# Last row group of a batch: one VectorE sum and one transposing matmul in place of nine accumulating matmuls

## The chip, the cores and the metric

The kernel runs on one core of a Trainium2 chip. Times are device microseconds of one execution. A run is one such time; beside it stands the span of an execution of that run, from its first to its last recorded instruction, and the mean TensorE clock that the records grant. "Tail" means here the last 10 us of the span, in which the last loads land and the final matmuls, scans and output run.

## The reference

`x` has 8 batches of 2048 rows of 4096 numbers, `w` has 4096.

```python
proj = (x @ w).squeeze(-1)                    # 8 x 2048 dot products
cm = np.maximum.accumulate(proj, axis=1)      # running maximum
is_record = (proj >= cm).astype(np.float32)
return np.cumsum(is_record, axis=1)           # running count of records
```

## The kernel before

268 MB of x are streamed once. VectorE (DVE) multiplies and sums the first 2816 columns of each row itself; GpSimd (POOL) multiplies the rest and ScalarE (ACT) sums it. TensorE (PE) adds the partial sums and turns them from a column (one row of x per partition) into a row (one batch per partition) by a matmul against the identity, accumulating in one PSUM tile `ps`. Then three VectorE operations make the maximum, the compare and the count.

The last 128 rows of batch 0 come in seven column pieces of falling size, so that little work is left when the last one lands. Each piece leaves its own 128x1 partial sum (the two pieces that POOL shares leave two).

```python
    PIECES = [   # batch, columns loaded, VectorE's columns, GpSimd's columns
        (1, 1408, D, (1408, VC), (VC, D)),
        (1, 0, 1408, (0, 1408), None),
        (0, 2816, D, (2816, 3328), (3328, D)),          # piece 2
        (0, 2048, 2816, (2048, 2816), None),
        (0, 1280, 2048, (1600, 2048), (1280, 1600)),    # piece 4
        (0, 832, 1280, (832, 1280), None),
        (0, 448, 832, (448, 832), None),
        (0, 160, 448, (160, 448), None),
        (0, 0, 160, (0, 160), None),                    # piece 8
    ]
    ...
        for i, (b, c0, c1, v, p) in enumerate(PIECES):
            ...
            piece(slot(B - 1 - b)[1], v, p, dst_v, dst_p, xq[i])
            if i == 1:
                parts += [(B, st_v, (sd, nv)), (B, b1x, None), (B, st_p, (pa, na))]
            elif b == 0:
                parts.append((1, dst_v, (sd, nv)))
                if p:
                    parts.append((1, dst_p, (pa, na)))

        a0 = next(i for i, q in enumerate(parts) if q[2] == (pa, na - 1))
        a1 = next(i for i, q in enumerate(parts) if q[2] == (pa, na))
        parts.insert(len(parts) - 2, parts.pop(a1))
        parts.insert(len(parts) - 4, parts.pop(a0))
        for k, (m, l, wait) in enumerate(parts):
            i = T.matmul(
                out=ps[:m, :P], lhsT=l[:, :m], rhs=identity,
                start=k == 0, stop=k == len(parts) - 1,
            )
            if wait:
                i._wait_ge(*wait)
        i.then_inc(psr, 1)
        scans(cm_l, rec_l, cnt_l, P, cm[:, N - 1 :], cnt[:, N - 1 :], 4)
        SY.dma_start(out=out[:, S0:], in_=cnt_l)._wait_ge(cs, NG + 2).then_inc(oe, 16)
```

TensorE's order of the twelve final parts is: three for all batches, then of batch 0 the pieces 2, 3, 4, 5, 6 (VectorE), piece 2 (ScalarE), piece 7, piece 4 (ScalarE), piece 8. `sd` counts VectorE's dots, `pa` ScalarE's sums.

Of the kernel before, what the change touches and what calls it, by code (L numbers as in the profile page):

```python
# [13 lines left out]
ALU = mybir.AluOpType  # L14
# [6 lines left out]
def kernel(  # L21
# [31 lines left out]
    PIECES = [  # L53
        (1, 1408, D, (1408, VC), (VC, D)),
        (1, 0, 1408, (0, 1408), None),
        (0, 2816, D, (2816, 3328), (3328, D)),
        (0, 2048, 2816, (2048, 2816), None),
        (0, 1280, 2048, (1600, 2048), (1280, 1600)),
# [3 lines that stand above are left out]
# [28 lines left out]
    def cut(n):  # L90
        off[0] += n
        assert off[0] <= 352
        return small[:, off[0] - n : off[0]]
# [1 line left out]
    sum_v, sum_p = cut(R * B), cut(R * B)  # L95
    st_v, st_p = cut(B), cut(B)
    b1x = cut(B)
    acc_v = cut(len(PIECES))
    acc_p = cut(len(PIECES))
    neg = cut(1)[:B]  # L100
    zero = ps[:B, WC - 1 :]

# [2 lines left out]
    def sem(name):  # L105
        return tc.alloc_semaphore(f"{name}_{next(ns)}")
# [6 lines left out]
    ws, idn, bw, wc, cs, od, oe, psr, pd, pl, go, sd, pa, con = (  # L113
        sem(n) for n in "ws idn bw wc cs od oe psr pd pl go sd pa con".split()
    )

    V, A, G, T, SY = nc.vector, nc.scalar, nc.gpsimd, nc.tensor, nc.sync

    def dot(xsl, wsl, dst):
        return V.tensor_tensor_reduce(  # L120
            out=xsl, in0=xsl, in1=wsl, scale=1.0, scalar=0.0,
            op0=ALU.mult, op1=ALU.add, accum_out=dst,
        )

    def add_up(xsl, dst):
        return A.activation(out=xsl, in_=xsl, func=ACTF.Copy, accum_out=dst)  # L126

    def w_pool(c0, c1):
        if c0 >= VC:
            return w_sb[:, c0 - VC : c1 - VC]  # L130
        assert W2 <= c0 and c1 <= W2 + WC
        return w2[:, c0 - W2 : c1 - W2]
# [15 lines left out]
    with tc.tile_critical(no_gpsimd_drain=True):  # L148

        for k in range(NK):  # L150
            g, t = divmod(k, B)
            i = SY.dma_start(
                out=xbuf[k % NS],
                in_=x[B - 1 - t, g * N : (g + 1) * N, :].rearrange(
                    "(p r) d -> p (r d)", r=R
                ),
            ).then_inc(xs[k % NS], 16)
            if k >= NS:
                i._wait_ge(fr[k % NS], 2 * (k // NS))
            if k == 0:  # L160
                A.dma_start(
                    out=w_row, in_=w.rearrange("(k c) one -> k (c one)", k=NW)
                ).then_inc(ws, 16)
            if t == NS and g:
                SY.dma_start(
                    out=out[:, (g - 1) * N : g * N], in_=cnt
                )._wait_ge(cs, g + 1).then_inc(od, 16)

        def slot(m):
            return m // R, xbuf[m // R][:, (m % R) * D : (m % R + 1) * D]  # L170
# [14 lines left out]
        for i, (b, c0, c1, _, _) in enumerate(PIECES):  # L185
            row_load(B - 1 - b, c0, c1, b, xq[i])
            if i == 3:
                SY.dma_start(
                    out=out[:, (NG - 1) * N : S0], in_=cnt
# [5 lines left out]
            out=identity, in_=identity, compare_op=ALU.not_equal, fill=1.0,  # L195
# [7 lines left out]
        for n, k in enumerate(order):  # L203
            c = k * WC
            dst = w_v[:, c : c + WC] if c < CV else ps
            i = T.matmul(  # L206
                out=dst, lhsT=identity[:NW, k : k + 1].to_broadcast([NW, P]),
                rhs=w_row, start=True, stop=True,
            ).then_inc(bw, 1)
# [21 lines left out]
        with V.Fori(0, NG):  # L231
# [3 lines left out]
            for t in range(B):  # L235
                b, s = B - 1 - t, t % NS
                V.wait_ge(xs[s], 16).then_inc(go, 1)
                V.sem_inc(xs[s], -16)  # L238
                for j in range(R):
                    i = dot(  # L240
                        xbuf[s][:, j * D : j * D + VC], w_v[:, :VC],
                        sum_v[:, j * B + b : j * B + b + 1],
                    )
# [3 lines left out]
        with G.Fori(0, NG):  # L247
            for t in range(B):
                s = t % NS
                for j in range(R):  # L250
                    xl = xbuf[s][:, j * D + VC : (j + 1) * D]
                    i = G.tensor_mul(out=xl, in0=xl, in1=w_sb).then_inc(pl, 1)  # L252
# [4 lines left out]
        with A.Fori(0, NG):  # L257
            for t in range(B):
                b, s = B - 1 - t, t % NS
                for j in range(R):  # L260
                    i = add_up(
                        xbuf[s][:, j * D + VC : (j + 1) * D],
                        sum_p[:, j * B + b : j * B + b + 1],
                    )._wait_ge(pl, j + 1)
# [5 lines left out]
        for g in range(NG):  # L270
            for j in range(R):
                for k, l in enumerate((sum_p, sum_v)):
                    i = T.matmul(  # L273
                        out=ps[:B, j:N:R], lhsT=l[:, j * B : (j + 1) * B],
                        rhs=identity, start=k == 0, stop=k == 1,
                    )
# [6 lines left out]
        nv = npool = na = 0  # L283
        parts = []

        def piece(xb, v, p, dst_v, dst_p, landed):
            nonlocal nv, npool, na
            dot(xb[:, v[0] : v[1]], w_v[:, v[0] : v[1]], dst_v)._wait_ge(
                landed, 16
            ).then_inc(sd, 1)  # L290
            nv += 1
            if p:
                xl = xb[:, p[0] : p[1]]
                G.tensor_mul(out=xl, in0=xl, in1=w_pool(*p))._wait_ge(  # L294
                    landed, 16
                ).then_inc(pl, 1)
                npool += 1
                add_up(xl, dst_p)._wait_ge(pl, npool).then_inc(pa, 1)
                na += 1
# [8 lines left out]
        for i, (b, c0, c1, v, p) in enumerate(PIECES):  # L308
            if b == 1:
                dst_v, dst_p = (b1x if p is None else st_v)[:, 1:2], st_p[:, 1:2]  # L310
            else:
                dst_v, dst_p = acc_v[:, i : i + 1], acc_p[:, i : i + 1]
            piece(slot(B - 1 - b)[1], v, p, dst_v, dst_p, xq[i])
            if i == 1:
                parts += [(B, st_v, (sd, nv)), (B, b1x, None), (B, st_p, (pa, na))]
            elif b == 0:
                parts.append((1, dst_v, (sd, nv)))
                if p:
                    parts.append((1, dst_p, (pa, na)))

        a0 = next(i for i, q in enumerate(parts) if q[2] == (pa, na - 1))
        a1 = next(i for i, q in enumerate(parts) if q[2] == (pa, na))
        parts.insert(len(parts) - 2, parts.pop(a1))
        parts.insert(len(parts) - 4, parts.pop(a0))
        for k, (m, l, wait) in enumerate(parts):
            i = T.matmul(  # L326
                out=ps[:m, :P], lhsT=l[:, :m], rhs=identity,
                start=k == 0, stop=k == len(parts) - 1,
            )
# [36 lines left out]
```

## Time and profile before

| | before |
|---|---|
| time, median of 3 runs | 631.44 us (631.29 to 631.71) |
| span of the profiled execution | 630.1 us |
| HBM traffic | 268 MB at 426 GB/s |
| busy: VectorE, GpSimd, TensorE | 64%, 59%, 5% |
| last dot's end to the cummax scan, in this trace | 1.70 us |

The timeline of the kernel before, at the end (start, length, engine, line, operation, output<-inputs, shapes, count, and in brackets the idle time before and who ended it). PEld is the weight load that goes with each pass of a matmul; an fp32 matmul here is two passes (24 recorded for the twelve final ones):

```profile
620.19 5.71 PE L326 MATMUL ps<-identity,small 128*8 128x128 f32 x24 [22.85 <-DVE small L120]
...
623.68 1.79 PEld L326 LDWEIGHTS ps<-identity,small 128*1 128x1 f32 x10 [0.39 <-DVE small L120]
...
623.92 0.32 DVE L120 CUSTOM_DVE_ANT_0 xall<-xall,w_v 128x160 f32<-128x160 f32 x1
624.16 0.08 DVE L120 DVE_READ_ACCUMULATOR2_ANT small<- 128x1 f32 x1
625.94 0.47 DVE L135 TENSOR_TENSOR_SCAN cm_l<-ps,cm,small 8x128 f32<-8x128 f32 x1 [1.70 <-PE ps L326]
626.45 0.28 DVE L139 TENSOR_TENSOR rec_l<-ps,cm_l 8x128 f32<-8x128 f32 x1
626.76 0.47 DVE L142 TENSOR_TENSOR_SCAN cnt_l<-rec_l,cnt,ps 8x128 f32<-8x128 f32 x1
627.26 0.31 SPq L334 DMA_DIRECT2D out_dram<-cnt_l  x1
```

The last dot is over at 624.24, but the scan starts 1.70 us later. In between PE works off a backlog: ten weight loads, so ten passes, so five matmuls, stand in a row from 623.68 on. Single passes taken from the trace start 0.213 us apart.

### The profile page before, as it was taken

Reading aid. Unit: us, or ns where it says so; the run is one execution under the profiler, and the core shown is the slowest. Engines: PE = TensorE matmul, PEld = TensorE weight load, DVE = VectorE, ACT = ScalarE, POOL = GpSimd, SP = SyncE. Lnnn points to the kernel's source line nnn. Section 1 sums busy time; section 2 is a strip of 40 time slices with the busy share of each in tenths; the row PEclk is TensorE's granted clock in tenths of the full one; section 3 lists DMA queues with packets and bytes.
Section 4 is the critical chain, followed back from the end, with each engine's and each line's share of the span. In section 5 each row is a group of like instructions: output and inputs, shape, how many; then the busy total and the mean of one; then the engine's idle time right before and its main releaser. Section 6 shows DMA issues by size and latency. Waiting matters only on the chain.

```text
span 630.1 us, 1239 instructions
## 1 busy us (share of the span) xinstructions
PE 33.4 (5%) x100; PEld 14.7 (2%) x100; DVE 406.2 (64%) x295; ACT 177.7 (28%) x262; POOL 369.2 (59%) x137
## 2 busy tenths in 40 slices
PE   8000000010000001000000010000001000000103
PEld 3000000000000000000000000000000000000001
DVE  0756666677655557766666675556667766555886
ACT  1322223233232222233232322222232322322332
POOL 0555666666555555666666555556666665555864
PEclk9999999999999999999999999999999999999999
DMA  9999999999999999999999999999999999999995
GB/s 385 415 446 443 412 443 444 422 434 440 424 437 441 431 427 443 440 415 446 438 421 440 440 424 437 440 425 434 440 440 418 443 440 418 444 437 417 425 431 209
DMA packets 8035, 268.55 MB, mean 426 GB/s; under 512 B 936, under 2 KB 1496, under 8 KB 2016
## 3 DMA queue, kind: packets, MB, share of 16 engines
q1 hardware_dynamic: 8016, 268.50, 98.7%
q8 instruction: 1, 0.02, 0.0%
q10 hardware_dynamic: 16, 0.02, 0.0%
q14 instruction: 2, 0.02, 0.0%
HBM read 268.45 MB, written 0.07 MB: 426 GB/s over the span
## 4 chain that ended last, share of the span: by engine, by line
POOL 52%; issue 38%; DMA 6%; PE 3%; DVE 0%; POOLq 0%; ACT 0%; SPq 0%; ACTq 0%
POOL xall L252 52%; DMA xall<-in_x_dram 6%; PE w_v L206 2%; PE ps L326 1%; PE ps L206 0%; DMA w<-in_w_dram 0%; DVE xall L120 0%; POOLq L255 0%; ACT w L216 0%; DVE cm_l L135 0%; DVE cnt_l L142 0%; SPq L176 0%; DVE rec_l L139 0%; ACT xall L126 0%; POOLq L247 0%
## 5 line engine op out<-in xcount | busy, mean ns | idle before, releaser
L120 DVE CUSTOM_DVE_ANT_0 xall<-xall,w_v 128x2816 f32<-128x2816 f32 (+3 forms) x135 | 389.3, 2931 | 185.8 <-DVEq L238 183.8
L252 POOL TENSOR_TENSOR xall<-xall,w_sb 128x1280 f32<-128x1280 f32 x120 | 345.2, 2903 | 246.0 <-POOLq L255 246.0
L126 ACT ACTIVATE xall<-xall 128x1280 f32<-128x1280 f32 x129 | 162.6, 1261 | 430.9 <-POOL xall L252 413.1
L273 PE MATMUL ps<-identity,small 128*8 128x128 f32 x60 | 13.6, 418 | 567.1 <-ACT xall L126 567.1
L294 POOL TENSOR_TENSOR xall<-xall,w_sb 128x1280 f32<-128x1280 f32 (+1 forms) x8 | 22.1, 2765 | 6.7 <-DMA xall<-in_x_dram 6.6
L126 ACT ACTIVATION_READ_ACCUMULATOR xall<-xall 128x1 f32 x129 | 24.0, 186 | 0.0
L273 PEld LDWEIGHTS ps<-identity,small 128*8 128x8 f32 x60 | 7.4, 130 | 574.4 <-ACT xall L126 570.6
L135 DVE TENSOR_TENSOR_SCAN cm<-ps,cm,small 8x384 f32<-8x384 f32 x6 | 6.0, 1004 | 15.0 <-PE ps L273 15.0
L206 PE MATMUL w_v<-w,identity 8*128 8x512 f32 x14 | 12.1, 1056 | 0.0
L224 DVE MEMSET ps<- 8x384 f32 x1 | 0.4, 378 | 17.1 <-ACT w L216 17.1
L120 DVE DVE_READ_ACCUMULATOR2_ANT small<- 128x1 f32 x135 | 11.0, 81 | 0.0
L326 PE MATMUL ps<-identity,small 128*1 128x128 f32 (+1 forms) x24 | 5.7, 407 | 22.9 <-DVE small L120 22.8
L142 DVE TENSOR_TENSOR_SCAN cnt<-rec,cnt,ps 8x384 f32<-8x384 f32 x6 | 6.0, 1002 | 0.2
L206 PEld LDWEIGHTS w_v<-w,identity 8*128 8x128 f32 x14 | 4.7, 333 | 7.3 <-issue 7.3
L213 ACT COPY w_sb<-w_v 128x768 f32<-128x768 f32 x1 | 0.8, 799 | 11.4 <-PE w_v L206 11.4
L139 DVE TENSOR_TENSOR rec<-ps,cm 8x384 f32<-8x384 f32 x6 | 3.3, 546 | 0.2
L326 PEld LDWEIGHTS ps<-identity,small 128*1 128x1 f32 (+1 forms) x24 | 2.1, 108 | 26.5 <-DVE small L120 25.0
L206 PE MATMUL ps<-w,identity 8*128 8x512 f32 x2 | 2.1, 1136 | 2.6 <-DMA w<-in_w_dram 2.6
L212 ACT ACT_TABLE_LOAD x1 | 1.3, 1283 | 1.6 <-SPq L148 1.6
L135 DVE TENSOR_TENSOR_SCAN cm_l<-ps,cm,small 8x128 f32<-8x128 f32 x1 | 0.5, 471 | 1.7 <-PE ps L326 1.7
L212 ACT COPY w_sb<-ps 128x512 f32<-128x512 f32 x1 | 0.6, 586 | 1.9 <-PE ps L206 1.9
L294 POOL TENSOR_TENSOR xall<-xall,w 128x320 f32<-128x320 f32 x1 | 0.9, 870 | 0.1
(15 smaller groups left out, 3.4 us busy)
## 6 DMA issues: line engine op xcount, KB each, us to landing
xall<-in_x_dram SPq DMA_DIRECT2D x40, 6144.0 KB, 47.8
xall<-in_x_dram SPq DMA_DIRECT2D x6, 2048.0 KB, 42.7
xall<-in_x_dram SPq DMA_DIRECT2D x1, 1344.0 KB, 36.7
xall<-in_x_dram SPq DMA_DIRECT2D x2, 384.0 KB, 30.5
xall<-in_x_dram SPq DMA_DIRECT2D x1, 704.0 KB, 38.1
xall<-in_x_dram SPq DMA_DIRECT2D x1, 640.0 KB, 39.1
xall<-in_x_dram SPq DMA_DIRECT2D x1, 224.0 KB, 21.7
xall<-in_x_dram SPq DMA_DIRECT2D x1, 192.0 KB, 21.8
```

Source lines behind the costliest of these rows:

```text
L120: return V.tensor_tensor_reduce(out=xsl, in0=xsl, in1=wsl, scale=1.0, scalar=0.0, op0=ALU.mult, op1=ALU.add, accum_out=dst,)
L126: return A.activation(out=xsl, in_=xsl, func=ACTF.Copy, accum_out=dst)
L135: V.tensor_tensor_scan(out=cm_, data0=ps[:B, :n], data1=neg.to_broadcast([B, n]), initial=cm0, op0=ALU.max, op1=ALU.max,)._wait_ge(psr, ba ...
L139: V.tensor_tensor(out=rec_, in0=ps[:B, :n], in1=cm_, op=ALU.is_ge)._wait_ge(psr, base + 1).then_inc(psr, 1)
L142: V.tensor_tensor_scan(out=cnt_, data0=rec_, data1=zero.to_broadcast([B, n]), initial=cnt0, op0=ALU.add, op1=ALU.add,)._wait_ge(psr, base ...
L206: i = T.matmul(out=dst, lhsT=identity[:NW, k : k + 1].to_broadcast([NW, P]), rhs=w_row, start=True, stop=True,).then_inc(bw, 1)
L212: A.copy(out=w_sb[:, CV - VC :], in_=ps)._wait_ge(bw, 1).then_inc(wc, 1)
L213: A.copy(out=w_sb[:, : CV - VC], in_=w_v[:, VC:CV])._wait_ge(bw, NW).then_inc(wc, 1)
L252: i = G.tensor_mul(out=xl, in0=xl, in1=w_sb).then_inc(pl, 1)
L273: i = T.matmul(out=ps[:B, j:N:R], lhsT=l[:, j * B : (j + 1) * B], rhs=identity, start=k == 0, stop=k == 1,)
L294: G.tensor_mul(out=xl, in0=xl, in1=w_pool(*p))._wait_ge(landed, 16).then_inc(pl, 1)
L326: i = T.matmul(out=ps[:m, :P], lhsT=l[:, :m], rhs=identity, start=k == 0, stop=k == len(parts) - 1,)
```

## The change

The intent is to take that backlog away. The eighteen slots for partial sums become one 128x18 tile, VectorE sums it to 128x1 once all are there, and one matmul adds the result to the three parts that stay. VectorE first waits for the last ScalarE sum; the wait stands ahead of the last dot.

```diff
-    acc_v = cut(len(PIECES))
-    acc_p = cut(len(PIECES))
+    accs = cut(2 * len(PIECES))
+    acc_v, acc_p = accs[:, : len(PIECES)], accs[:, len(PIECES) :]
+    fin = cut(1)
 ...
+            if i == len(PIECES) - 1:
+                V.wait_ge(pa, na)
             piece(slot(B - 1 - b)[1], v, p, dst_v, dst_p, xq[i])
             if i == 1:
                 parts += [(B, st_v, (sd, nv)), (B, b1x, None), (B, st_p, (pa, na))]
-            elif b == 0:
-                parts.append((1, dst_v, (sd, nv)))
-                if p:
-                    parts.append((1, dst_p, (pa, na)))
-
-        a0 = ...      # (the four lines that put the two ScalarE parts late)
+        V.tensor_reduce(
+            out=fin, in_=accs, op=ALU.add, axis=mybir.AxisListType.X
+        )._wait_ge(sd, nv).then_inc(sd, 1)
+        nv += 1
+        parts.append((1, fin, (sd, nv)))
```

More of the change, by code (lines that the diff above doesn't have):

```diff
@@ L315 @@
                 parts += [(B, st_v, (sd, nv)), (B, b1x, None), (B, st_p, (pa, na))]
-            elif b == 0:
-                parts.append((1, dst_v, (sd, nv)))
-                if p:
-                    parts.append((1, dst_p, (pa, na)))
-        a0 = next(i for i, q in enumerate(parts) if q[2] == (pa, na - 1))
-        a1 = next(i for i, q in enumerate(parts) if q[2] == (pa, na))
-        parts.insert(len(parts) - 2, parts.pop(a1))
-        parts.insert(len(parts) - 4, parts.pop(a0))
+        V.tensor_reduce(
[3 more added lines that the diff above has]
+        parts.append((1, fin, (sd, nv)))
         for k, (m, l, wait) in enumerate(parts):
```

## The prediction

> **What bounds the kernel.** The page shows the 16 DMA engines at 9 tenths in 39 of 40 slices, 426 GB/s over a 630.1 us span; DVE is busy 64%, PE 5%. For about 620 us the kernel streams x, and the change touches none of that. It can only act in the tail. The chain of waits reads there: last DVE dots, PE at the final-projection line (ps), three DVE scan operations, output DMA.
>
> **The tail (timeline).** DVE runs the six last dots nearly without a gap from 620.96; the accumulator read of the last one (128x160) ends at 624.24. PE has 12 final matmuls of two passes each (24 recorded); queued passes start 0.213 us apart, so a matmul costs 0.427 us. From 623.68 to the end PE is busy without a break with five of them: piece 6, the two PoolE/ScalarE parts placed late, piece 7, piece 8. The last two passes start at 625.34 and 625.56; the cummax scan starts at 625.94, 1.70 us after the last dot (the waits view gives the same). Scan, compare and scan take 1.3 us, and the output DMA is issued at 627.26.
>
> **What the change does.** PE keeps 4 of 12 matmuls (8 passes); the first three wait for data ready by about 621.1 and are done by about 622. [...] the last one stands behind its backlog. That backlog goes. Added: one VectorE sum over 128x18. Estimate from this trace: dots of 160 and 2816 elements (0.317 and 3.08 us) give 1.04 ns per element and 0.15 us fixed; a 128x1 accumulator read costs 0.08 us. So 0.10 to 0.17 us, plus 0.04 us for the same-engine semaphore (gap between scan and compare).
>
> New tail: last dot ends 624.24; sum from 624.28 to 624.42; PE starts 0.05 us later (as 622.55 to 622.61 today); two passes 0.17 us apart when none queues before them (622.61, 622.78); last pass start to scan 0.38 us as today. The scan starts at about 625.03 instead of 625.94: 0.9 us gained, all of it on the critical path, because what follows is a serial chain.
>
> **The added wait.** Ahead of the last dot VectorE waits for the last ScalarE sum, which ends at 623.43; the last dot starts at 623.92. About 0.5 us of slack: it should cost nothing. In the loop such a wait takes 21 ns, and a dot follows within some 0.2 us.
>
> **Prediction.** 631.44 - 0.9 = 630.55 us, range 630.15 to 631.0. Faster by over 2%: 0.5%; within 2%: 99%; slower by over 2%: 0.5%. The gain is 0.14%: the tail is a small part of the span.
>
> **What would show it.** Matmul passes at the final-projection line fall from 24 to 8, PE idle for some 2 us ahead of the last pair; a VectorE reduce of 128x18 of 0.10 to 0.17 us right behind the last dot; the cummax scan's wait for PE shrinks from 1.70 to about 0.6 us; the last dot still ends 3.3 us after its run of dots began.
>
> **What would make it wrong.** The explicit wait keeps VectorE from queueing the last dot early and delays it by 0.2 us or more; the sum costs 0.3 us or more; PE, idle for 2 us, runs its last pair slower (after 23 us idle today it still started passes 0.21 us apart, so I do not expect it); or the difference drowns in the scatter of runs (0.42 us here) or in a small shift of the loads.

## More of the kernel before

From the page of the kernel before, the busy tenths in 40 equal slices of the span, first the granted TensorE clock, then the DMA engines:

```profile
PEclk9999999999999999999999999999999999999999
DMA  9999999999999999999999999999999999999995
```

The loads set the pace for all but the last slice, so a change of the final matmuls acts in the tail only.

## The result, and the profile after

| | before | after |
|---|---|---|
| time, median of 4 runs | 631.39 us (631.29 to 631.71) | 631.33 us (631.24 to 631.52) |
| span of the profiled execution | 630.1 us | 629.3 us |
| last dot's end to the scan, in the traces | 1.70 us | 0.89 us |

The ratio after to before is 0.9996, 95% interval 0.9982 to 1.0010. The gain is 0.06 us by the medians, where 0.9 was predicted. The predicted range, 630.15 to 631.0, is missed, although the trace has the gain almost to the digit.

The timeline of the changed kernel, the same stretch as above:

```profile
620.04 1.61 PE L326 MATMUL ps<-identity,small 128*8 128x128 f32 x6 [22.87 <-DVE small L121]
...
623.87 0.32 DVE L121 CUSTOM_DVE_ANT_0 xall<-xall,w_v 128x160 f32<-128x160 f32 x1
624.11 0.08 DVE L121 DVE_READ_ACCUMULATOR2_ANT small<- 128x1 f32 x1
624.22 0.17 DVE L319 TENSOR_REDUCE small<-small 128x1 f32<-128x18 f32 x1
624.45 0.09 PEld L326 LDWEIGHTS ps<-identity,small 128*1 128x1 f32 x2 [3.30 <-DVE small L319]
624.45 0.59 PE L326 MATMUL ps<-identity,small 128*1 128x128 f32 x2 [2.81 <-DVE small L319]
625.08 0.47 DVE L136 TENSOR_TENSOR_SCAN cm_l<-ps,cm,small 8x128 f32<-8x128 f32 x1 [0.68 <-PE ps L326]
625.58 0.28 DVE L140 TENSOR_TENSOR rec_l<-ps,cm_l 8x128 f32<-8x128 f32 x1
625.89 0.47 DVE L143 TENSOR_TENSOR_SCAN cnt_l<-rec_l,cnt,ps 8x128 f32<-8x128 f32 x1
626.39 0.31 SPq L334 DMA_DIRECT2D out_dram<-cnt_l  x1
```

Every step is as predicted: the sum took 0.17 us, PE had been idle for 2.8 us and started its pair at once, the scan started at 625.08 (625.03 was predicted), and the output DMA was issued at 626.39 instead of 627.26, 0.87 us earlier (0.81 of it is the shorter wait; the last dot itself ended 0.05 earlier). The extra wait cost nothing: the last dot started as soon as the one before it was done. So the question is not what the change did to the trace, but why the timed executions of the kernel before were not 0.9 us slower. The page of the changed kernel, moreover, has no clock row at all.

### The profile page after: what moved, and what is told of

Same layout as the page of the kernel before. It is cut to its first block, busy times and chain, and to the rows that moved or that the text cites. A ratio compares the mean times of both kernels' runs of the same rounds, so it can differ in the third digit from the quotient of the medians.

```text
span 629.3 us, 1209 instructions
## 1 busy us (share of the span) xinstructions
PE 29.8 (5%) x84; PEld 13.0 (2%) x84; DVE 406.4 (65%) x296; ACT 177.7 (28%) x262; POOL 369.1 (59%) x137
## 4 chain that ended last, share of the span: by engine, by line
POOL 53%; issue 39%; DMA 4%; PE 3%; DVE 1%; POOLq 0%; ACT 0%; SPq 0%; ACTq 0%
POOL xall L253 53%; DMA xall<-in_x_dram 3%; PE w_v L207 2%; PE ps L274 0%; DVE xall L121 0%; PE ps L207 0%; DMA w<-in_w_dram 0%; DVE cm L136 0%; DVE cnt L143 0%; POOLq L256 0%; PE ps L326 0%; ACT w L217 0%; DVE rec L140 0%; DVE cm_l L136 0%; DVE cnt_l L143 0%
## 5 line engine op out<-in xcount | busy, mean ns | idle before, releaser
L326 PE MATMUL ps<-identity,small 128*8 128x128 f32 (+1 forms) x8 | 2.2, 404 | 25.7 <-DVE small L121 22.9
```

The source lines that it names most:

```text
L326: i = T.matmul(out=ps[:m, :P], lhsT=l[:, :m], rhs=identity, start=k == 0, stop=k == len(parts) - 1,)
```

## The experiments

Two questions in turn. First: does the time follow the end of the trace (T1), or does something outside it, at the start or the end of the program, take the gain back (T2)? Then, when the run lists were in: does the TensorE clock differ between executions (theory C), or do the loads or an instruction fetch jitter (rival J)? Executions of before are quoted one by one from the run lists. All results were correct but for the one noted.

### 1. after_again: the changed kernel, unaltered

> The changed kernel unaltered, five rounds against before on one chip. Theory T1 (the trace tells the time, and the first comparison hid the gain in scatter or between chips): it is 0.8 to 0.9 us faster than before, as the profiled spans are (629.3 against 630.1). Theory T2 (something outside the chain of the trace decides when the clock of the timed run stops, or starts, and takes the gain back): within 0.2 us of before, while its profiled span is 0.8 to 0.9 us shorter.

Measured, five rounds on one chip: 631.35 us (631.14 to 631.41) against 631.85 us (631.19 to 632.32, 9 runs), ratio 0.9992 (0.9978 to 1.0006). Neither expectation: half the gain is there. The scatter tells more. The changed kernel stays within 0.27 us, the kernel before spreads over 1.13 us, its best runs level with the changed kernel and its worst 0.9 us behind.

### 2. after_pad2 and after_pad5: the tail made longer by known amounts

```diff
+        for _ in range(2):                # 5 in after_pad5
+            nv += 1
+            V.memset(rec, 0.0)._wait_ge(sd, nv).then_inc(sd, 1)
         nv += 1
         parts.append((1, fin, (sd, nv)))
```

> The changed kernel with two serial VectorE memsets of 8x384 between the sum and its matmul, 0.38 us each plus some 0.04 us: the tail gets 0.84 us longer and its span is that of before again. T1: 0.84 us slower than the changed kernel, so within 0.1 us of before. T2: the same time as the changed kernel and as before, 631.3 us, since a tail shorter than that of before is worth nothing.

> Five such memsets: span 2.1 us longer than the changed kernel. T1: 2.1 us slower than the changed kernel, 1.2 us slower than before. T2 with a floor at the time of before: 1.2 us slower than before and than the changed kernel. T2 with a step larger than 2 us somewhere: no difference or a jump.

Measured: 632.46 us and 633.75 us, so 1.11 and 2.40 us over the unaltered changed kernel on the same chip; the spans of the profiled executions (630.4 and 631.8 against 629.4) grew by 0.99 and 2.38 us. A memset with its wait cost 0.5 us, not the 0.42 I had put down. The time follows the trace one to one: no floor and no step, T2 falls. (after_pad2 was not level with before, as T1 had it, but slower; before on this chip was no fixed quantity.)

### 3. before_pad2: the same pad in the kernel before

```diff
+        V.memset(rec, 0.0)._wait_ge(psr, 4).then_inc(psr, 1)
+        V.memset(rec, 0.0)._wait_ge(psr, 5).then_inc(psr, 1)
-        scans(cm_l, rec_l, cnt_l, P, cm[:, N - 1 :], cnt[:, N - 1 :], 4)
+        scans(cm_l, rec_l, cnt_l, P, cm[:, N - 1 :], cnt[:, N - 1 :], 6)
```

> The kernel before with two such memsets between its last matmul and the last scans: span 0.84 us longer than before. T1: 0.84 us slower. T2 with a floor just at the time of before: 0.84 us slower too. T2 with a slack beyond before (an event that comes later than the end of the tail): less than 0.3 us slower.

Measured: 632.73 us (632.52 to 633.29), 0.88 us over before. The kernel before has no slack either. What differs must lie in its own executions.

After these four the run lists showed a group pattern: the clock stood at 0.998, 0.622 or 1.0 from one execution of before to the next, and the spans went with it. That gave theory C: 0.213 us between passes is not the full clock but half of it; the tail of before keeps TensorE busy so long that in some executions the clock is lifted in the middle of the backlog, which then takes half the time.

A trace in hand already shows the first half of that. Of after_pad5 (the windows view: stretch, then busy time and count by engine, granted clock, DMA share, GB/s):

```profile
core 0: us, PE busy (x) PEld busy (x) DVE busy (x) ACT busy (x) POOL busy (x), PEclk, DMA share, GB/s
620.00:621.70 1.70, 1.56 (x6) 0.47 (x6) 1.49 (x5) 1.04 (x2) 1.68 (x1) 0.50 1.03 397
```

Its six passes take 1.56 us at a recorded clock of 0.50; the same six took 1.61 us in the changed kernel, whose records hold no clock at all (the small difference is the wait between the fourth and the fifth). The first four weight loads take 0.53 us in both, and the last pair 0.59 us in both; queued passes of the changed kernel start 0.213 us apart, as those of before do. So the changed kernel's trace, which has no record of the clock, had run at the pace of the recorded 0.50: the 1.0 of the views is filled in there, not measured.

### 4. before_again: the kernel before, unaltered

> The kernel before unaltered, to see its executions one by one with span and granted clock. Theory C (the TensorE clock): passes 0.213 us apart are the half-rate clock, and in some executions the long run of matmuls in the tail lifts the clock to full rate before the backlog is worked off. Then executions fall in groups: those in which no full-rate period is recorded ahead of the last pass have spans of 630.0 to 630.4 us and times near 632.1, those in which it starts 1 to 2.5 us earlier have spans of 629.1 to 629.8 and times of 631.2 to 631.8. Rival J (jitter of the loads, or of an instruction fetch that only the trace of before shows in the tail): spans scatter without regard to the clock, and the pass spacing is 0.213 us in every trace.

Measured: 631.76 us (631.28 to 632.20). The profiled execution fell on a fast one, 631.28 us with a span of 629.2. Its timeline:

```profile
623.77 0.96 PEld L326 LDWEIGHTS ps<-identity,small 128*1 128x1 f32 x10 [0.39 <-DVE small L120]
...
624.01 0.32 DVE L120 CUSTOM_DVE_ANT_0 xall<-xall,w_v 128x160 f32<-128x160 f32 x1
624.25 0.08 DVE L120 DVE_READ_ACCUMULATOR2_ANT small<- 128x1 f32 x1
625.06 0.47 DVE L135 TENSOR_TENSOR_SCAN cm_l<-ps,cm,small 8x128 f32<-8x128 f32 x1 [0.73 <-PE ps L326]
```

Against the trace of before above: the same ten weight loads, so the same five matmuls, take 0.96 us instead of 1.79. The passes of the backlog are 0.109 us apart, and the trace has a record of clock 1.0 from 623.43 to 626.85 and of 0.5 after it. The scan starts 0.73 us after the last dot: sooner than in the changed kernel, 0.89. In the trace that I had read for the prediction, the record of 1.0 starts at 625.70, just after the last pass (625.56), too late to help. The starts of these records are read from the packed traces; a view shows only their ends, because it fills in 1.0 where there is no record. The fast trace first, then the slow one:

```profile
core 0: us, PE busy (x) PEld busy (x) DVE busy (x) ACT busy (x) POOL busy (x), PEclk, DMA share, GB/s
626.00:627.00 1.00, 0.00 (x0) 0.00 (x0) 0.35 (x1) 0.00 (x0) 0.00 (x0) 0.92 0.00 0
627.00:629.20 2.20, 0.00 (x0) 0.00 (x0) 0.00 (x0) 0.00 (x0) 0.00 (x0) 0.50 0.01 2
...
629.00:630.10 1.10, 0.00 (x0) 0.00 (x0) 0.00 (x0) 0.00 (x0) 0.00 (x0) 0.55 0.00 0
```

In both traces the record of 1.0 is 3.41 us long, called a step below. Rival J does not tell the two apart: the last dot ended at 624.24 in the slow trace and at 624.33 in the fast one, and the instruction fetch in the tail stands in the fast trace (624.35) as well as in the slow one (623.55).

All 41 executions of before in the lists of the five-round runs (four lists of nine on three chips, and this kernel's own five), by span. (A single one beside the runs of experiment 10, 631.97 us with a span of 629.8 and a clock of 0.622, falls in the middle group.)

| span, us | executions | time, us | mean | clock as listed |
|---|---|---|---|---|
| up to 629.5 | 15 | 631.09 to 631.59 | 631.32 | 0.998 in 8, 0.999 or 1.0 in 6, 0.622 in 1 |
| 629.6 to 629.9 | 13 | 631.37 to 632.07 | 631.77 | 0.622 in 11, 0.711 and 0.998 in one each |
| 630.0 and over | 13 | 632.05 to 632.88 | 632.36 | 0.999 or 1.0 in 12, 0.617 in 1 |

0.998 is what a lift at 623.4 gives: clock 0.5 for the last 2.4 us of 629.2, and 1.0 filled in elsewhere. It occurs in nine executions, none of them in the slow third. 1.0 alone tells nothing, for the reason above; fast executions have it too.

The listed 0.622 can be read as well, by an estimate, and it accounts for 11 of the 13 in the middle group. I take it to belong to executions in which the clock was also lifted after each of five earlier bursts of matmuls, at 133.63 us and every 116 us from there in the trace of after_pad5. That trace has no step of full clock in the tail (0.50 in every window from 618 to 628) and lists 0.619; that of before_warm3_look has the same five early lifts and six steps of 3.41 us in the tail, and lists 0.636. A step adds 0.0027 (half of 3.41 us in 630), so 0.622 is one step in the tail. When it came is not recorded; that it came in the middle of the backlog is my guess, from spans (629.6 to 629.9) that lie between those of the other two groups. The unaltered changed kernel lists 0.619 or 0.620 where before lists 0.622: no step in its tail.

### 5. before_idle4: no long busy stretch ahead of the backlog

```diff
+        parts = parts[:3] + parts[7:]     # wrong result on purpose: pieces 2 to 5 left out
         for k, (m, l, wait) in enumerate(parts):
```

> The kernel before without the matmuls of pieces 2 to 5 (VectorE parts), so a wrong result on purpose: the last five matmuls and their backlog stay, but TensorE idles from about 621.8 to 623.7 us[...]. Theory C: the clock is not lifted in time in any execution; passes of the last five are 0.213 us apart, the scan starts 1.65 to 1.75 us after the last dot, spans 630.0 to 630.5 and times 632.0 to 632.5 in all executions, with a scatter of at most 0.5 us, where before itself reaches down to 631.1. Rival J: same groups as before, down to 631.1.

Measured, five executions: 632.03, 632.26, 632.27, 632.54, 632.59 us; before on the same chip 631.22 to 632.88, five of nine under 631.5. So the times reach 0.09 us past what theory C expected, and none is fast. (The chip's comparison called the result correct: the count did not notice the missing parts. It is wrong all the same.) From its timeline:

```profile
623.82 1.79 PEld L327 LDWEIGHTS ps<-identity,small 128*1 128x1 f32 x10 [2.43 <-DVE small L120]
623.82 2.29 PE L327 MATMUL ps<-identity,small 128*1 128x128 f32 x10 [1.94 <-DVE small L120]
...
624.30 0.08 DVE L120 DVE_READ_ACCUMULATOR2_ANT small<- 128x1 f32 x1
626.15 0.47 DVE L135 TENSOR_TENSOR_SCAN cm_l<-ps,cm,small 8x128 f32<-8x128 f32 x1 [1.77 <-PE ps L327]
```

Four matmuls fewer, and slower: TensorE idles for 1.94 us ahead of the backlog, ten loads take 1.79 us again, the scan waits 1.77 us, and the fast group is gone. This is what the prediction took the kernel before to be in all its executions. One of its executions has the five early lifts and lists 0.619, so, by the same reading, it had no step of full clock in the tail. Rival J has no reason for it; the trace does not even have the instruction fetch, and is slow all the same.

### 6. after_8more: the changed kernel with the instruction count of before

```diff
         for g in range(NG):
+            if g == 2:
+                for _ in range(8):
+                    T.matmul(
+                        out=ps[32:64, :P], lhsT=identity[:, :32], rhs=identity,
+                        start=True, stop=True,
+                    )
```

> The changed kernel with 8 useless matmuls about 300 us earlier, so that TensorE's instruction count is that of before and the instruction fetch comes back. Rival J in its form of the instruction fetch: the fetch shows up again near the end, and times scatter from 631.2 to 632.3. Theory C: the fetch may come back, the times stay at 631.1 to 631.5 as those of the changed kernel.

Measured: 631.47 us (631.13 to 631.66); the fetch did not come back. So this run says little of the fetch; the times stayed in one group, as C has it.

### 7. before_warm, after_warm: TensorE kept busy ahead of the tail, first try

Useless matmuls, gated by VectorE's count of dots, write to PSUM partitions that nothing reads:

```diff
+        def keep_busy(n, cols, count):
+            for q in range(n):
+                i = T.matmul(
+                    out=ps[32:64, :cols], lhsT=identity[:, :32],
+                    rhs=w_sb[:, :cols], start=True, stop=True,
+                )
+                if q == 0:
+                    i._wait_ge(sd, count)
+        keep_busy(4, WC, nr - 1)          # nr = 6 full rows; WC = 512
+        keep_busy(2, WC, nr)
         for k, (m, l, wait) in enumerate(parts):
+            if k == len(parts) - 1:       # after_warm only: up to the last dot
+                keep_busy(1, 256, nr + 3)
+                for c in range(4, 9):
+                    keep_busy(2 if c < 8 else 1, P, nr + c)
```

> The kernel before, with useless matmuls from the fifth row's dot on (about 612 us) into a part of the PSUM bank that nothing reads, so that TensorE is busy for 8 us ahead of the final matmuls. Theory C: full clock recorded in the tail, passes about 0.107 us apart, no backlog at the last dot, wait of the cummax scan for PE 0.4 to 0.7 us instead of 1.70; every execution at 630.9 to 631.3 us with a scatter under 0.4 us. Rival J: same scatter as before (631.2 to 632.3), passes still 0.213 us apart; or slower, since PE has more to do.

> The changed kernel with such matmuls kept up until the last dot. Theory C: the final two passes are some 0.1 us apart and end earlier; the scan starts 0.65 to 0.75 us after the last dot instead of 0.89; 0.15 to 0.25 us faster than the changed kernel (631.1 to 631.2), and no better than the kernel before with the clock kept up, by 0.1 to 0.3 us. Rival J: the same as the changed kernel or slower.

Measured: before_warm 632.48 us (631.40 to 633.31), after_warm 631.89 us (631.35 to 632.34), before beside them 632.09 us (631.09 to 632.66). Both missed as to the times. The profiled executions, each the fastest of its five, did show the expected tails: passes 0.109 us apart, scan 0.73 and 0.68 us after the last dot. In before_warm the lift came at 618.12, 6 us after the filling began, in after_warm at 615.83, 3.8 us after (there the weight loads stand 0.85 us apart up to 615.45 and 0.43 from 616.07 on). Where it comes early or late this filling runs out or runs over; that this made the slow ones is likely, but their traces were not taken.

### 8. before_warm2, after_warm2, early_warm: a filling that was too thick

The filling begun at 603 us, as `(6, 2), (6, 3), (6, 4), (8, 5), (3, 6), (3, 7)` matmuls of 512 columns and dot counts. `early_warm` also moves the two ScalarE parts:

```diff
-        parts.insert(len(parts) - 2, parts.pop(a1))
-        parts.insert(len(parts) - 4, parts.pop(a0))
+        parts.insert(len(parts) - 4, parts.pop(a1))
+        parts.insert(len(parts) - 6, parts.pop(a0))
```

> The kernel before with useless matmuls that fill TensorE from 603 to 620 us, mended: the first try filled too little once the clock was up and too much while it was down. Theory C: full clock in every execution from 610 us at the latest to the end, passes about 0.109 us apart, scan 0.73 us after the last dot, all times 631.1 to 631.5 as in the best executions of before. Rival J: 631.1 to 632.6 as before.

> The changed kernel with the same filling, kept up to the last dot. Theory C: scan 0.68 us after the last dot instead of 0.885, all times 631.0 to 631.4: 0.1 to 0.25 us faster than the changed kernel and within 0.1 us of the kernel before filled the same way, so that at full clock the change is worth nothing or nearly nothing.

> The kernel before, filled the same way, with the two PoolE/ScalarE parts moved two places forward in TensorE's order, so that at full clock nothing queues at the last dot. Theory C: scan 0.40 to 0.50 us after the last dot (sum 0.28 us saved against the changed kernel at full clock), times 630.8 to 631.1, the fastest of all versions by 0.2 us or more.

Measured: 640.16, 641.62 and 640.09 us (four, five and four executions), 9 to 10 us slower than before. This was a slip of mine, and it shows in one line of early_warm's timeline:

```profile
602.86 27.99 PE L327 MATMUL ps<-w_sb,identity 128*32 128x512 f32 x61 [5.70 <-DVE small L120]
...
630.27 0.60 PE L337 MATMUL ps<-identity,small 128*8 128x128 f32 x4
```

61 passes took 28 us and pushed the first final matmul to 630.27: I had counted one pass per matmul. Useless as tests; a filler that overruns costs all that it overruns.

### 9. before_warm3, after_warm3, early_warm3, after_third: the filling mended

```diff
+        for n, cols, c in (
+            (3, WC, 2), (3, WC, 3), (3, WC, 4), (4, WC, 5), (3, 256, 6), (3, 256, 7)
+        ):
+            keep_busy(n, cols, c)
```

> The kernel before, TensorE kept busy from 603 us on with about half as many useless matmuls as in the last try, which by a slip of mine filled twice the time there was (one pass of 128x512 took 0.429 us at full clock, two passes per matmul) and so pushed the final matmuls 9 us back. Theory C: full clock by 610 us in every execution, passes 0.109 us apart, scan 0.73 us after the last dot, all times 631.1 to 631.5. Rival J: 631.1 to 632.9 as before.

> The changed kernel with the same mended filling up to the last dot. Theory C: scan 0.68 us after the last dot instead of 0.885, all times 631.0 to 631.4, that is 0.1 to 0.25 us faster than the changed kernel and within 0.15 us of the kernel before filled the same way: at full clock the change is worth next to nothing.

> The kernel before, filled the same way, with the two PoolE/ScalarE parts moved two places forward in TensorE's order, so that at full clock nothing queues at the last dot. Theory C: scan 0.40 to 0.50 us after the last dot, times 630.8 to 631.1, the fastest of all versions by 0.2 us or more.

> The changed kernel unaltered, on the chip of these three, as their measure. Theory C: its final pair always runs at half clock (0.17 us apart, after an idle stretch), so 631.1 to 631.5 with no groups, whatever before does beside it.

Measured on one chip, sorted:

| kernel | five executions, us | median |
|---|---|---|
| before (9 runs) | 631.20 to 632.35, five under 631.5 | 631.49 |
| before_warm3 | 631.43 631.50 631.51 632.05 632.18 | 631.51 |
| after_third | 631.24 631.24 631.25 631.30 631.43 | 631.25 |
| after_warm3 | 631.24 631.56 631.59 632.21 632.42 | 631.59 |
| early_warm3 | 630.91 631.20 631.21 631.26 631.65 | 631.21 |

The timeline of before_warm3:

```profile
623.89 0.96 PEld L339 LDWEIGHTS ps<-identity,small 128*1 128x1 f32 x10 [0.39 <-DVE small L120]
...
624.37 0.08 DVE L120 DVE_READ_ACCUMULATOR2_ANT small<- 128x1 f32 x1
625.18 0.47 DVE L135 TENSOR_TENSOR_SCAN cm_l<-ps,cm,small 8x128 f32<-8x128 f32 x1 [0.73 <-PE ps L339]
```

That of after_warm3, with the sum in it:

```profile
624.34 0.08 DVE L121 DVE_READ_ACCUMULATOR2_ANT small<- 128x1 f32 x1
624.45 0.17 DVE L319 TENSOR_REDUCE small<-small 128x1 f32<-128x18 f32 x1
624.68 0.38 PE L343 MATMUL ps<-identity,small 128*1 128x128 f32 x2
625.10 0.47 DVE L136 TENSOR_TENSOR_SCAN cm_l<-ps,cm,small 8x128 f32<-8x128 f32 x1 [0.47 <-PE ps L343]
```

And that of early_warm3, in which only piece 8's own pair is left to load behind the last dot:

```profile
624.37 0.08 DVE L120 DVE_READ_ACCUMULATOR2_ANT small<- 128x1 f32 x1
624.51 0.09 PEld L339 LDWEIGHTS ps<-identity,small 128*1 128x1 f32 x2 [0.16 <-DVE small L120]
624.93 0.47 DVE L135 TENSOR_TENSOR_SCAN cm_l<-ps,cm,small 8x128 f32<-8x128 f32 x1 [0.47 <-PE ps L339]
```

The tails are as expected to 0.01 us: from last dot to scan 0.73, 0.68 and 0.47 us. So at full clock the change is worth 0.05 us of tail, and moving two parts in TensorE's order is worth 0.26. But "every execution" was wrong for both filled kernels: two of five each were 0.5 us or more longer. The filling seems to have a price besides: the last dot ended at 624.42 to 624.45 in these three traces and at 624.33 in after_third on the same chip (over all traces, at 624.40 to 624.53 with a filling and at 624.12 to 624.38 without). after_third held: one narrow group, beside a before that spreads from 631.20 to 632.35. early_warm3 missed its 630.8 to 631.1 us in four of five executions: it is level with the changed kernel by the medians (631.21 against 631.25) and has the fastest execution of all, 630.91, but five runs don't separate them; a version that clearly beats both kernels was not found.

### 10. after_warm3_look, before_warm3_look: one more trace each

> One more look at the changed kernel with TensorE filled, in the hope of a trace of one of its slow executions (2 of 5 had spans of 630.1 and 630.3 instead of 629.3 to 629.5). If it falls among them, theory C expects in it passes at half rate somewhere in the tail (a later lift, or a drop back), with the useless matmuls queueing in front of the final pair; else (rival) full rate throughout and the last dot itself later by 0.6 us or more, from the loads or from slower dots. If it falls among the fast ones, it repeats 0.68 us from last dot to scan and tells nothing more.

> The same look at the kernel before with TensorE filled (2 of 5 executions had spans of 630.0 instead of 629.4 to 629.7). If slow: theory C expects half-rate passes in the tail, the rival a later last dot at full rate. If fast: 0.73 us from last dot to scan again.

Measured: 631.41 and 631.52 us, both fast executions, scan 0.68 and 0.73 us after the last dot again. What the long executions of the filled kernels are stays open. One can be read a little further from the run list: after_warm3's 632.42 us lists a clock of 0.633, by the estimate of experiment 4 five steps of full clock in the tail, where its 631.59 us lists 0.636, six. That is 3.41 us less of full clock, as theory C expects; where the missing step lay is not recorded, and the other three long ones list 0.999 or 1.0, which cannot be read so.

## Why the prediction was wrong, point by point

- **Loads set the time, only the tail can change: right.** The paddings moved time and span by the same amount.
- **What the change removes and adds: right, in the execution that the trace shows.** Sum 0.17 us (0.10 to 0.17), scan at 625.08 (625.03), extra wait free, 0.87 us gained between the two traces (0.9).
- **"PE has 12 final matmuls ... a matmul costs 0.427 us" and "PE, idle for 2 us, runs its last pair slower (after 23 us idle today it still started passes 0.21 us apart, so I do not expect it)": this is the step that failed.** The figure was right for this trace, the reading of it as TensorE's normal pace was not. 0.213 us between passes goes with the half clock (0.50 is recorded in after_pad5), 0.109 with the full one (1.0 is recorded in before_again). TensorE was slow before and after the 23 us of idleness (passes 0.213 us apart at 595 us as well as at 621 us in that trace), so "no slower than today" proved nothing. In some executions of before the clock rises in time, within the long tail (at 623.43 in before_again): then the backlog costs 0.73 us from last dot to scan. In others it rises too late (at 625.70 in the trace of before): then it costs 1.70. What lifts it is not settled here. That the long busy stretch of TensorE does is my inference from four traces: from 620 to 624 us TensorE was busy for 3.72 us in before_again and 3.80 in before, whose records of 1.0 begin at the two moments named; it was busy for 1.74 us in before_idle4, whose backlog of ten loads took 1.79 us to the end, and for 1.60 in the changed kernel, whose trace has no record. The changed kernel's last pair took 0.59 us there and in after_pad5 (recorded clock 0.50), against 0.38 in after_warm3; in every trace of it without filling the scan came 0.88 to 0.89 us after the last dot where nothing was padded.
- **"631.44 - 0.9": the mis-sized term.** 1.70 us of tail belongs to executions near 632.2: the 41 listed executions of before have times 1.75 to 2.18 us over their spans, and the trace I read has a span of 630.1. (Its own time is not on record; any of the comparison's times would be only 1.2 to 1.6 us over that span.) The median that I subtracted from, 631.44, and all runs of that comparison (631.29 to 631.71) lie in the fast and middle groups. For a slow execution the rule works: mean of the slow third 632.36, changed kernel 631.31 (mean of 14 executions in three comparisons, 631.14 to 631.52). For the fast third there is nothing to gain: 631.32.
- **What the change is worth:** over all 41 and 14 executions, 631.79 - 631.31 = 0.48 us, under 0.1%, and a narrower spread. This is a mean over chips: the three comparisons give 0.06, 0.50 and 0.24 us by their medians, and the interval of the ratio, about 0.14% to each side, contains 1 in all three. "Within 2%" was never in doubt.
- **How it could have been seen.** The trace that I read for the prediction lists a clock of 0.999, and its windows view grants 0.55 in the last 1.1 us: the clock was not the same throughout, while the row shows nines. I believed the clock row of the profile instead.

Shown: that both paces occur in traces of the same unaltered kernel, with the recorded clock to match; that without a long busy stretch only the slow group is left (before_idle4); that the time follows the tail. Inferred: that the busy stretch lifts the clock, and that the lift explains each of the 41 executions. Only one of them has a trace (the one read for the prediction is not among them); for the 12 that list 0.622, the step in the tail is an estimate from the listed clock, and its moment a guess. Open: the long executions of the filled kernels.

## What to carry to other kernels

When an engine is nearly idle in the profile, check its pace by the start-to-start spacing of instructions against that of a trace whose clock is recorded (here 0.213 us at 0.50 and 0.109 at 1.0) before costing its work, and don't take a filled-in clock row for a measurement. The short burst of matmuls at the end of this memory-bound kernel ran at half or at full clock from one execution to the next (1.70 and 0.73 us from last dot to scan); a trace is one draw, so compare its span with the spread of timed runs before subtracting from their median. Taking matmuls off TensorE can also go with a slower pace of the rest: the changed kernel's last pair took 0.59 us, and 0.38 where useless matmuls filled TensorE ahead of it.

## Spacings measured in this case

- fp32 passes of 128x128 start 0.213 us apart in the trace of before and 0.109 at full clock (ten of them took 2.29 us in before_idle4 and 1.25 in before_warm3). Passes of 128x512 start 0.85 us apart in early_warm up to 605.42 us and 0.43 from 606.23 on. There were two passes per matmul.
- The 16 passes that open the kernel (8x512, stationary and moving operand of 8 partitions) keep PE busy for 14.0 us on end in the traces of before and after: from the second on they start 0.853 us apart, to the last, and neither trace has a record of full clock there. The cause was not tested.
- VectorE's sum of 128x18 fp32 took 0.172 us in the trace of after.
- The times of this one program fall into groups, by span: 631.1 to 631.6, 631.4 to 632.1 and 632.05 to 632.9 us.
